# Spreading the expert gates with one single-pass matmul a token, its operands built four tokens at a time

## The chip, the cores and the metric

The kernel runs on one core of one Trainium2 chip. The metric is the device time of one execution in microseconds (us), lower is better. A profile is one execution taken by the hardware profiler; its span is counted from the first to the last instruction. Engines are named as in the profile: PE is TensorE's matmul, PEld its weight load, DVE is VectorE, ACT is ScalarE, POOL is GpSimd and SP is the engine that issues most DMAs.

## What is computed

Three layers over 256 tokens of width 2048. The change lies in the last one, a mixture of 16384 experts, each a row of `u` and a row of `v`. An expert has two keys of 128 values, and each of eight heads picks 16 experts for a token:

```python
cand_s = (v_half[:, :, 0, :, None] + v_half[:, :, 1, None, :]).reshape(T, PEER_HEADS, K * K)
cand_i = (i_half[:, :, 0, :, None] * PEER_N_KEYS + i_half[:, :, 1, None, :])...
top_s, pick = lax.top_k(cand_s, K)
experts = jnp.take_along_axis(cand_i, pick, axis=-1)
gates = jax.nn.softmax(top_s, axis=-1)
...
a = jnp.einsum('cd,ced->ce', hc, w_u[ec]).astype(F32)
coef = (gc * jax.nn.gelu(a)).astype(dt)
return jnp.einsum('ce,ced->cd', coef, w_v[ec])
```

All inputs are float32, and the 128 picks of a token (8 heads by 16) are spread over all 16384 experts.

## The kernel before

The kernel doesn't gather experts. It computes `gelu(h u)` for all of them, multiplies by a dense table of gates that is zero for experts not picked, and multiplies by all of `v`.

**Weights.** A unit of weights is a tile of 128 x 2048 floats, loaded by SP into `raw` (3 buffers). `wsplit` (lines 199 to 230) splits it in two pieces of 1024 columns into an exact high part `whi` (ACT, L210) and a low part `wlo` (DVE, L211), with three buffers for each. Every product is three matmuls on those parts (`mm3`, L289 to L291 for `u`, L285 to L287 for `v`). `wsplit` traces its instructions at high priority.

**Order of the last layer.** The function `peer` works in two halves of the second key (`hf`). A half takes 64 units of `u`, then `apply_gates` for eight blocks of eight units, then 64 units of `v`. The result tiles of the first half fill the slots that the second half's `u` needs, so no unit of the second half comes before the `v` products of the first.

**Spread work.** During the `u` units of the first half a generator `spread` runs in steps, five steps for four units: first `topk`, which leaves `gsel`, a tile [128, 3, 256] with gate, first key and second key of each pick, picks in the partitions and tokens along the columns; then `scatter`, 32 steps of eight tokens. A step's instructions are queued behind the newest split (ACT, DVE) and the newest product (PE) by `anchored`; POOL has no such anchor. Engines take their instructions in the order in which the scheduler of the framework left them.

**Scatter.** For each token it builds two 128 x 128 matrices: on DVE (L1351) a one at the first key of each pick times the gate, on POOL (L1354) a one at the second key. A float32 matmul of one by the other (L1363) sums the picks into a 128 x 128 table in PSUM. Four tokens share a bank; ACT (L1365) copies it into the tile `sg`, and after 16 tokens SP writes `sg` to `gd` in DRAM (L1367). `apply_gates` reads `gd` back by blocks of experts (L1373) and multiplies on POOL (L1377). `coefficients` then splits the result into high and low parts (L1476 on ACT, L1477 on DVE) for the `v` products.

Of the kernel before, what the change touches and what calls it, by code (L numbers as in the profile page):

```python
# [10 lines left out]
F32 = mybir.dt.float32  # L11
# [9 lines left out]
P = 128  # L21
# [7 lines left out]
# columns of the packed per-partition vectors  # L29
V_PRE = 0            # norm_pre, 2 x 16  # L30
V_BQ = 32            # b_q_norm, 2 x 4
V_BKV = 40           # b_kv_norm, 2 x 2
V_BADA = 44          # b_ada, 96
V_GMIX = 140         # g_norm_mix, 16
V_GFFN = 156         # g_norm_ffn, 16
V_PEK = 172          # cmp_pe_k, 16 (j) x 2 (parity)
V_PEV = 204          # cmp_pe_v
V_N = 236

# columns of the packed constants  # L40
C_COSA = 0           # 2 x 128
C_SINA = 256
C_COSB = 512         # 2 x 64
C_SINB = 640
C_CMP = 768          # 2 x 240
C_ROW = 1248         # 2 (rows of the query tiles that see a compressed block)
C_BLK = 1250         # 4
C_IOTA = 1254        # 128
# [3 lines left out]
class Kern:  # L52
# [36 lines left out]
    @contextmanager  # L89
    def phase(self, name, ntmp):  # L90
        """a pool for the temporaries of one phase"""
        self.ntmp = ntmp
        with self.tc.tile_pool(name=name, bufs=1) as self.xp:
            yield
# [9 lines left out]
    def constants(self, lo, hi, eng=None):  # L104
        """the columns lo..hi of the packed constants; returns a way to name them"""
        t = self.xp.tile([P, hi - lo], F32, tag="con", name=self.name("con"))
        (eng or self.nc.gpsimd).dma_start(t, self.a["con"][:, lo:hi])
        return lambda c, n: t[:, c - lo : c - lo + n]

# [1 line left out]
    # prep: generators, a step a unit; heads: generators of three stages, run as a pipeline.  # L111
    # Each step goes behind the newest split of weights and the newest product, so that
    # its inputs are there by the time that the engines come to it.
    def behind(self, *ins):
        """queues what follows behind these instructions, each on its own engine"""
        e = ExitStack()
        for i in ins:
            e.enter_context(self.tc.issue_after(i.ins))
        return e
# [31 lines left out]
    def need(self, key):  # L151
        """runs what is left of the spread work until a result is there"""
        while key not in self.done:
            assert self.prep or self.heads or self.live, key
            self.prep_step()
            self.heads_step()

# [1 line left out]
    def rsqrt(self, out, x, scale, n, eps=EPS):  # L159
        """out = 1/sqrt(x*scale + eps) for [P, n]: a guess from the bits, then Newton steps"""  # L160
# [33 lines left out]
    def wsplit(self, ap, n=2048):  # L194
        """a unit of weights as exact high and low parts, in pieces of at most 1024 columns"""
# [57 lines left out]
    def ada_plan(self, rate, stop):  # L253
        """so many units of the modulation for each unit of weights, up to a number"""
# [6 lines left out]
    def ada_vec(self, i, tag):  # L261
        """mod part i, [128, 16]: feature k*128+p at [p, k]"""
# [6 lines left out]
    def row_bcast(self, out, v, *qs):  # L269
        """out[p, k*128+f] = v[f, k] for every p"""  # L270
# [22 lines left out]
    def proj_tok(self, hT, units, width, evac, kt=KT, early=False, before={}):  # L293
        """token-major: out[t, c] for one chunk of columns; units hold several k tiles"""
# [19 lines left out]
    def proj_feat_by_k(self, hT, units, evac):  # L314
        """feature-major: 512 columns; a unit holds four k tiles, so that it starts before all of hT is there"""
# [12 lines left out]
    def proj_feat(self, hT, units, evac):  # L328
        """feature-major: out[c, t] for 128 columns a unit; two units a bank"""
# [12 lines left out]
    def transposes(self, ps, blocks):  # L342
        """in this order"""
# [6 lines left out]
    # ================= the first two layers =================  # L350
# [3 lines left out]
    def chunk_stats(self, st, m, c, src):  # L354
        """the sum of the squares of a chunk of 512 columns"""
# [3 lines left out]
    def norm_stats(self, r, st, m):  # L359
        """r[:, m] = 1/rms of the rows of tile m from the sums over chunks"""  # L360
# [14 lines left out]
    def start(self, x):  # L375
        """the first loads, in the order of their use"""
# [12 lines left out]
    def layer1(self, l, x, rx, dma=None):  # L389
# [7 lines left out]
        def features(c):  # L397
            """4 tiles of hT; behind the last, the sums that 1/rms needs"""
# [58 lines left out]
        def tables():  # L457
            # rope tables with the gains folded in; 1/rms of x as a row over the tokens
# [45 lines left out]
        qk = [self.S(10 + m, [P, D]) for m in range(2)]   # q 1024, k 256, v 256 (A), v 512 (C)  # L504
# [3 lines left out]
        def a_heads(m, src, nh, h0, ti):  # L508
            """1/rms of nh heads into rqa[:, m, h0:], rope into a temporary"""
# [16 lines left out]
        self.prep_step()  # L526
        kv = self.S(12, [P, 2, 2, 512])      # k_nope (4 x 128), v (4 x 128)
# [39 lines left out]
        qT = self.S(4, [P, 2, 4, T])     # nope parts, then rope parts in the first 64 partitions  # L567
# [5 lines left out]
        def b_prep():  # L573
            # rope on the 64 rope columns of each head and on the shared key
# [189 lines left out]
    def gate(self, m, ps, half_r, src, oT, c):  # L764
        """silu(r*ps) * src, transposed into 4 feature tiles of oT; half_r holds r/2"""
# [21 lines left out]
    def rope(self, dst, src, cos, sin, nh, q):  # L787
        """dst = src*cos + swap(src)*sin on [P, nh, 4q]; swap exchanges neighbouring runs of q"""
# [14 lines left out]
    def softmax_pv(self, scores, sc, scp, vs, out, key):  # L803
        """two heads of 256 keys: out[:, 128*j] = softmax(s_j * scale) @ v_j"""
# [38 lines left out]
    # ================= the last layer: mixer =================  # L843
    def modulated(self, x, rx, g, shift, slots):
        """(x/rms * g + shift) transposed, in high and low parts"""
# [25 lines left out]
    def gain(self, i, vcol, tag):  # L871
        """g * (1 + scale)"""
# [7 lines left out]
    def layer2(self, x, rx):  # L880
# [29 lines left out]
        KTt = self.S(12, [P, 4, 2, T])       # k_c, v_c, k_s, k_w; feature-major  # L910
# [234 lines left out]
        def retain(h2):  # L1145
# [19 lines left out]
            pv = po.rearrange("p (c d) -> p c d", c=4)       # (tile, head)  # L1165
# [89 lines left out]
    # ================= the last layer: experts =================  # L1255
    def topk(self, sh, tk, gsel):
        """the 16 best experts of each head, in steps for the time of other work;
        gates and both key indices go to gsel with (head, k) in the partitions"""
# [73 lines left out]
    def top16(self, row, v, i):  # L1332
        """the 16 largest of a row in order, and their indices; the row is spoilt"""
# [7 lines left out]
    def scatter(self, gsel, gd):  # L1341
        """one-hot rows by one-hot columns, summed over (head, k); a step is 8 tokens"""
        nc = self.nc
        sg = None
        for t0 in range(0, T, 4):
            if t0 % 16 == 0:
                sg = self.S(12 + t0 // 16 % 2, [P, P, 16])
            oh = [self.tmp(tag="oh", bufs=5), self.tmp(tag="oh1", bufs=5)]
            for j in range(4):
                w, t = slice(j * P, (j + 1) * P), slice(t0 + j, t0 + j + 1)  # L1350
                nc.vector.tensor_scalar(  # L1351
                    oh[0][:, w], self.io, gsel[:, 1, t], gsel[:, 0, t], op0=ALU.is_equal, op1=ALU.mult
                )
                nc.gpsimd.tensor_scalar(oh[1][:, w], self.io, gsel[:, 2, t], None, op0=ALU.is_equal)  # L1354
            self.scatter_mm(gd, t0, oh, sg)
            if t0 % 8 == 4:
                yield
    def scatter_mm(self, gd, t0, oh, sg):
        nc = self.nc
        ps = self.pt()  # L1360
        for j in range(4):
            w = slice(j * P, (j + 1) * P)
            nc.tensor.matmul(ps[:, w], oh[0][:, w], oh[1][:, w], start=True, stop=True)  # L1363
        t = t0 % 16
        nc.scalar.copy(sg[:, :, t : t + 4], ps.rearrange("p (t i) -> p i t", t=4))  # L1365
        if t == 12:
            nc.sync.dma_start(gd[t0 // 16], sg.rearrange("p i t -> p (i t)"))  # L1367

    def apply_gates(self, gd, b, A):
        """multiplies 8 tiles of experts by their gates"""  # L1370
# [8 lines left out]
    def peer(self, x, rx, out):  # L1379
# [42 lines left out]
        # gates by (first key, second key) for every token  # L1422
# [7 lines left out]
        for hf in range(2):  # L1430
# [41 lines left out]
            def coefficients(b, j):  # L1472
                ch = self.tmp(dt=F32R, tag="oh", bufs=5)
                cl = self.tmp(dt=F32R, tag="oh1", bufs=5)
# [10 lines left out]
            def finish(n, ms=(0, 1)):  # L1485
                w = slice(n * 512, n * 512 + 512)
                for m in ms:
                    if hf == 0:
                        # the sum of this half, kept until the other is there
# [15 lines left out]
            for b in range(8):  # L1505
                if hf == 1 and b in (1, 3):
                    # x + gate * (the sum of the first half)
# [14 lines left out]
            # the last units by chunks, so that the chunks end one after another  # L1522
# [215 lines left out]
```

## Time and profile before

| | us |
|---|---|
| median of three runs | 3018.02 |
| lowest and highest | 3017.7, 3020.57 |
| span of the profiled execution | 3020.2 |

No time outside the span is given for the profiled execution; its span lies 2.2 us above the median of the runs. In the profile a row of an engine's groups gives the line, the engine, what is written and read, the count, the busy time, the mean of one instruction, and the idle time of the engine in front of it with what ended it. A wait that an engine has while another sets the pace costs nothing.

### The profile page before, as it was taken

Reading aid. Unit: us, or ns where it says so; the run is one execution under the profiler, and the core shown is the slowest. Engines: PE = TensorE matmul, PEld = TensorE weight load, DVE = VectorE, ACT = ScalarE, POOL = GpSimd, SP = SyncE. Lnnn points to the kernel's source line nnn. Section 1 sums busy time; section 2 is a strip of 40 time slices with the busy share of each in tenths; the row PEclk is TensorE's granted clock in tenths of the full one; section 3 lists DMA queues with packets and bytes.
Section 4 is the critical chain, followed back from the end, with each engine's and each line's share of the span. In section 5 each row is a group of like instructions: output and inputs, shape, how many; then the busy total and the mean of one; then the engine's idle time right before and its main releaser. Section 6 shows DMA issues by size and latency. Waiting matters only on the chain.

```text
span 3020.2 us, 45455 instructions
## 1 busy us (share of the span) xinstructions
PE 2942.8 (97%) x18244; PEld 2631.1 (87%) x18244; DVE 1982.9 (66%) x3152; ACT 1366.1 (45%) x1903; POOL 408.1 (14%) x404
## 2 busy tenths in 40 slices
PE   9999989999989999999999998999999999999998
PEld 7798878898879998879999998888889999977886
DVE  6877767867666667856888665655546655555555
ACT  6444445544453455444444444344444443444443
POOL 0000000000030000011018994200000101011001
PEclk9999999999989999999999999999999999999999
DMA  7767757677757656654555557655558677555554
GB/s 277 262 224 287 264 189 269 228 262 280 264 183 273 237 203 226 227 205 162 179 182 182 207 212 237 223 191 185 191 191 294 246 254 264 214 202 209 184 192 139
DMA packets 131955, 672.08 MB, mean 223 GB/s; under 512 B 11200, under 2 KB 44112, under 8 KB 56480
## 3 DMA queue, kind: packets, MB, share of 16 engines
q1 hardware_dynamic: 128384, 650.94, 60.6%
q0 software_dynamic: 3360, 18.24, 1.6%
q8 instruction: 144, 2.36, 0.3%
q14 instruction: 67, 0.55, 0.0%
HBM read 639.77 MB, written 29.36 MB: 222 GB/s over the span
## 4 chain that ended last, share of the span: by engine, by line
PE 88%; DVE 5%; POOL 2%; DMA 2%; issue 2%; ACT 1%; SPq 0%; ACTq 0%; DVEq 0%; POOLq 0%
PE ps L286 16%; PE ps L287 16%; PE ps L285 16%; PE ps L291 11%; PE ps L289 11%; PE ps L290 10%; DVE wlo L211 2%; PE ps L346 2%; DMA raw<-in_wada 2%; PE ps L1363 2%; POOL S L1313 1%; PE ps L833 1%; POOL tmp L1354 1%; ACT whi L210 1%; PE ps L644 0%
## 5 line engine op out<-in xcount | busy, mean ns | idle before, releaser
L211 DVE TENSOR_TENSOR wlo<-raw,whi 128x1024 fp32r<-128x1024 f32 (+2 forms) x950 | 1202.3, 1271 | 800.4 <-ACT whi L210 798.4
L210 ACT CAST whi<-raw 128x1024 fp32r<-128x1024 f32 (+2 forms) x950 | 984.0, 1037 | 1331.0 <-PE ps L287 662.5
L291 PE MATMUL ps<-S,wlo 128*128 128x256 f32 x3072 | 871.5, 284 | 17.2 <-DVE wlo L211 17.0
L289 PE MATMUL ps<-S,whi 128*128 128x256 f32 x3072 | 878.4, 286 | 1.3 <-ACT whi L210 1.3
L290 PE MATMUL ps<-S,whi 128*128 128x256 f32 x3072 | 869.9, 283 | 0.0
L291 PEld LDWEIGHTS ps<-S,wlo 128*128 128x128 f32 x3072 | 590.1, 192 | 19.7 <-DVE wlo L211 19.6
L289 PEld LDWEIGHTS ps<-S,whi 128*128 128x128 f32 x3072 | 590.1, 192 | 6.2 <-issue 4.3
L290 PEld LDWEIGHTS ps<-S,whi 128*128 128x128 f32 x3072 | 590.3, 192 | 0.4
L285 PE MATMUL ps<-whi,S 128*128 128x512 f32 (+3 forms) x1264 | 488.5, 387 | 0.7 <-ACT S L781 0.7
L286 PE MATMUL ps<-wlo,S 128*128 128x512 f32 (+3 forms) x1264 | 482.4, 382 | 3.6 <-DVE wlo L211 3.4
L287 PE MATMUL ps<-whi,S 128*128 128x512 f32 (+3 forms) x1264 | 482.1, 382 | 0.2 <-DVE S L782 0.2
L286 PE MATMUL ps<-wlo,tmp 128*128 128x512 f32 x1024 | 405.4, 396 | 7.4 <-DVE wlo L211 7.3
L285 PE MATMUL ps<-whi,tmp 128*128 128x512 f32 x1024 | 405.1, 396 | 0.0
L287 PE MATMUL ps<-whi,tmp 128*128 128x512 f32 x1024 | 405.0, 395 | 0.0
L286 PEld LDWEIGHTS ps<-wlo,S 128*128 128x128 f32 x1264 | 239.6, 190 | 46.7 <-DVE wlo L211 5.0
L285 PEld LDWEIGHTS ps<-whi,S 128*128 128x128 f32 x1264 | 239.3, 189 | 45.0 <-issue 3.0
L287 PEld LDWEIGHTS ps<-whi,S 128*128 128x128 f32 x1264 | 239.0, 189 | 44.6 <-DVE S L782 0.6
L249 DVE SCALAR_TENSOR_TENSOR raw<-raw,S 128x2048 f32<-128x2048 f32 x96 | 219.6, 2288 | 55.1 <-DMA raw<-in_wada 54.9
L286 PEld LDWEIGHTS ps<-wlo,tmp 128*128 128x128 f32 x1024 | 192.5, 188 | 55.3 <-DVE wlo L211 9.1
L285 PEld LDWEIGHTS ps<-whi,tmp 128*128 128x128 f32 x1024 | 192.5, 188 | 46.3
L287 PEld LDWEIGHTS ps<-whi,tmp 128*128 128x128 f32 x1024 | 192.5, 188 | 46.3
L1354 POOL TENSOR_SCALAR tmp<-con,gsel 128x128 f32<-128x128 f32 x256 | 192.8, 772 | 11.0 <-DVE gsel L1329 7.4
(248 smaller groups left out, 1957.6 us busy)
## 6 DMA issues: line engine op xcount, KB each, us to landing
raw<-in_win SPq DMA_DIRECT2D x136, 1024.0 KB, 5.1
raw<-in_u SPq DMA_DIRECT2D x128, 1024.0 KB, 4.9
raw<-in_v SPq DMA_DIRECT2D x120, 1024.0 KB, 4.9
raw<-in_wada SPq DMA_DIRECT2D x96, 1024.0 KB, 5.0
raw<-in_wout SPq DMA_DIRECT2D x48, 1024.0 KB, 4.9
raw<-in_wq SPq DMA_DIRECT2D x16, 1024.0 KB, 4.9
gd<-S SPq DMA_DIRECT2D x16, 1024.0 KB, 4.5
S<-gd SPq DMA_DIRECT2D x16, 1024.0 KB, 8.3
```

The costliest lines, as they stand in the source:

```text
L210: ia = nc.scalar.copy(hi[:, :h], raw[:, c : c + h])
L211: iv = nc.vector.tensor_sub(lo[:, :h], raw[:, c : c + h], hi[:, :h])
L249: nc.vector.scalar_tensor_tensor(raw, raw, 0.5, self.cact, op0=ALU.mult, op1=ALU.mult, accum_out=self.mod[:, u : u + 1])
L285: mm(out, ah, wh, start=first, stop=False)
L286: mm(out, ah, wl, start=False, stop=False)
L287: self.last_mm = mm(out, al, wh, start=False, stop=last)
L289: mm(out, wh, ah, start=first, stop=False)
L290: mm(out, wh, al, start=False, stop=False)
L291: self.last_mm = mm(out, wl, ah, start=False, stop=last)
L346: t = self.nc.tensor.transpose(ps[:, i * P : (i + 1) * P], b, self.ident)
L1354: nc.gpsimd.tensor_scalar(oh[1][:, w], self.io, gsel[:, 2, t], None, op0=ALU.is_equal)
L1363: nc.tensor.matmul(ps[:, w], oh[0][:, w], oh[1][:, w], start=True, stop=True)
```

## The change

`scatter` gives its matrices other contents and builds them four tokens at a time. The gate is first split into two parts, `hi` rounded to the short float32 form that the matmul takes in one pass, and the rest. Rows are now plain ones at the first key (DVE, 128 x 512 for four tokens), `cols` plain ones at the second key (DVE, 128 x 512). The columns are multiplied by the first gate part on DVE and by the second on POOL (two instructions of 128 x 256 on each), side by side. A token's matmul is then 128 columns of rows by 256 columns, in the form `F32R`. A bank holds two tokens with two sums each; ACT copies one half into `sg` and DVE adds the other to it (128 x 256 each, two of each for four tokens). `scatter_mm` is gone. The tag `oh1` has four buffers where it had five, in `coefficients` too. All other changed lines are comments.

```diff
     def scatter(self, gsel, gd):
...
         nc = self.nc
+        gp = self.xp.tile([P, 2, T], F32, tag="gp", name="gp")
+        hi = self.tmp(dt=F32R, tag="oh", bufs=5)[:, :T]
+        nc.scalar.copy(hi, gsel[:, 0])
+        nc.scalar.copy(gp[:, 0], hi)
+        nc.vector.tensor_tensor(gp[:, 1], gsel[:, 0], gp[:, 0], op=ALU.subtract)
+        io = self.io.rearrange("p (o k) -> p o k", o=1).to_broadcast([P, 4, P])
...
         sg = None
         for t0 in range(0, T, 4):
             if t0 % 16 == 0:
                 sg = self.S(12 + t0 // 16 % 2, [P, P, 16])
-            oh = [self.tmp(tag="oh", bufs=5), self.tmp(tag="oh1", bufs=5)]
-            for j in range(4):
-                w, t = slice(j * P, (j + 1) * P), slice(t0 + j, t0 + j + 1)
-                nc.vector.tensor_scalar(
-                    oh[0][:, w], self.io, gsel[:, 1, t], gsel[:, 0, t], op0=ALU.is_equal, op1=ALU.mult
-                )
-                nc.gpsimd.tensor_scalar(oh[1][:, w], self.io, gsel[:, 2, t], None, op0=ALU.is_equal)
-            self.scatter_mm(gd, t0, oh, sg)
+            ts = slice(t0, t0 + 4)
+            rows = self.tmp(dt=F32R, tag="oh", bufs=5)
+            cols = self.tmp(tag="oh1", bufs=4)
+            parts = [self.tmp(dt=F32R, tag=g, bufs=n) for g, n in (("oh", 5), ("oh1", 4))]
+            nc.vector.tensor_tensor(
+                rows.rearrange("p (t k) -> p t k", t=4), io, over(gsel[:, 1, ts]), op=ALU.is_equal
+            )
+            cv = cols.rearrange("p (t k) -> p t k", t=4)
+            nc.vector.tensor_tensor(cv, io, over(gsel[:, 2, ts]), op=ALU.is_equal)
+            for h in range(2):
+                pv = parts[h].rearrange("p (t e k) -> p t e k", t=2, e=2)
+                for e, eng in enumerate((nc.vector, nc.gpsimd)):
+                    g = gp[:, e, t0 + 2 * h : t0 + 2 * h + 2].rearrange("p (t o) -> p t o", o=1)
+                    eng.tensor_tensor(pv[:, :, e], cv[:, 2 * h : 2 * h + 2], g.to_broadcast([P, 2, P]), op=ALU.mult)
+            t = t0 % 16
+            for h in range(2):
+                ps = self.pt()
+                for j in range(2):
+                    nc.tensor.matmul(
+                        ps[:, j * T : (j + 1) * T], rows[:, (2 * h + j) * P : (2 * h + j + 1) * P],
+                        parts[h][:, j * T : (j + 1) * T], start=True, stop=True,
+                    )
+                pv = ps.rearrange("p (t e i) -> p i t e", t=2, e=2)
+                out = sg[:, :, t + 2 * h : t + 2 * h + 2]
+                nc.scalar.copy(out, pv[:, :, :, 0])
+                nc.vector.tensor_tensor(out, pv[:, :, :, 1], out, op=ALU.add)
...
             if t0 % 8 == 4:
                 yield
-    def scatter_mm(self, gd, t0, oh, sg):
-        nc = self.nc
-        ps = self.pt()
-        for j in range(4):
-            w = slice(j * P, (j + 1) * P)
-            nc.tensor.matmul(ps[:, w], oh[0][:, w], oh[1][:, w], start=True, stop=True)
-        t = t0 % 16
-        nc.scalar.copy(sg[:, :, t : t + 4], ps.rearrange("p (t i) -> p i t", t=4))
...
             def coefficients(b, j):
                 ch = self.tmp(dt=F32R, tag="oh", bufs=5)
-                cl = self.tmp(dt=F32R, tag="oh1", bufs=5)
+                cl = self.tmp(dt=F32R, tag="oh1", bufs=4)
```

## Rows read from the trace of the kernel before

**Rows 1.** The page's busy times, share of the span in brackets.

```profile
PE 2942.8 (97%) x18244; PEld 2631.1 (87%) x18244; DVE 1982.9 (66%) x3152; ACT 1366.1 (45%) x1903; POOL 408.1 (14%) x404
```

**Rows 2.** Busy time by stretch, from the gates' arrival to the first `v` product.

```profile
core 0: us, PE busy (x) PEld busy (x) DVE busy (x) ACT busy (x) POOL busy (x), PEclk, DMA share, GB/s
1631.00:1839.00 208.00, 207.67 (x1764) 207.10 (x1764) 138.16 (x311) 95.20 (x130) 192.80 (x256) 1.00 0.57 211
...
1631.00:1904.00 273.00, 262.33 (x2193) 261.16 (x2193) 176.30 (x333) 118.05 (x157) 218.18 (x262) 0.97 0.62 219
```

**Rows 3.** Groups by line and shape, 1630 to 1840 us.

```profile
L1354 POOL TENSOR_SCALAR tmp<-con,gsel 128x128 f32<-128x128 f32 x256 | 192.8, 772 | 11.0 <-DVE gsel L1329 7.4 <-PE ps L1363 3.6
L1351 DVE TENSOR_SCALAR tmp<-con,gsel 128x128 f32<-128x128 f32 x256 | 78.8, 369 | 2.6 <-PE ps L1363 2.6
L211 DVE TENSOR_TENSOR wlo<-raw,whi 128x1024 fp32r<-128x1024 f32 x53 | 65.0, 1226 | 67.2 <-ACT whi L210 67.2
L1365 ACT COPY S<-ps 128x512 f32<-128x512 f32 x64 | 36.1, 587 | 8.7 <-PE ps L1363 8.7
```

**Rows 4.** The chain that ended last, two steps of the scatter (start, us, what).

```profile
1662.13 1.78 PE ps L1363 x16
1669.67 1.78 PE ps L1363 x16
```

**Rows 5.** Timeline of PE at the end of the first half's `u`.

```profile
1901.77 0.28 PE L289 MATMUL ps<-S,whi 128*128 128x256 f32 x1
1901.89 0.28 PE L290 MATMUL ps<-S,whi 128*128 128x256 f32 x1
...
1903.56 0.40 PE L285 MATMUL ps<-whi,tmp 128*128 128x512 f32 x1
```

**Rows 6.** Two-input DVE groups of the whole run, by line and shape.

```profile
L1268 DVE TENSOR_TENSOR S<-S 128x256 f32<-128x256 f32 x16 | 6.4, 415 | 0.0
L1239 DVE TENSOR_TENSOR S<-S,tmp 128x512 f32<-128x512 f32 x8 | 5.5, 688 | 0.1
L1153 DVE TENSOR_TENSOR tmp<-ps,S 128x256 f32<-128x256 f32 x8 | 3.3, 414 | 0.0
```

**Rows 7.** Instructions of POOL's L1313, a two-input multiply of 128 x 256.

```profile
L1313 POOL TENSOR_TENSOR S<-S,S x32: 728/1167/2785, 1577.5 to 1623.1; 128x256 f32<-128x256 f32 x32
```

**Rows 8.** Timeline of DVE and POOL while POOL runs sixteen of L1313.

```profile
1575.04 2.29 DVE L1305 TENSOR_TENSOR S<-S,con 128x2048 f32<-128x2048 f32 x1
...
1582.27 2.72 DVE L1305 TENSOR_TENSOR S<-S,con 128x2048 f32<-128x2048 f32 x1
1584.91 5.12 DVE L211 TENSOR_TENSOR wlo<-raw,whi 128x1024 fp32r<-128x1024 f32 x3
...
1577.47 20.02 POOL L1313 TENSOR_TENSOR S<-S,S 128x256 f32<-128x256 f32 x16 [207.55 <-DVE S L1305]
```

**Rows 9.** Timeline from the last write of the gates to their use.

```profile
1839.23 0.33 SPq L1367 DMA_DIRECT2D gd<-S  x1
...
1853.99 5.69 POOL L1377 TENSOR_TENSOR S<-S,S 128x2048 f32<-128x2048 f32 x1 [26.38 <-ACT whi L210]
...
1859.72 2.18 ACT L1476 CAST tmp<-S 128x512 fp32r<-128x512 f32 x4 [5.78 <-POOL S L1377]
...
1860.05 4.56 POOL L1377 TENSOR_TENSOR S<-S,S 128x2048 f32<-128x2048 f32 x1 [0.36 <-DMA S<-gd]
...
1860.37 10.89 DVE L1477 TENSOR_TENSOR tmp<-S,tmp 128x512 fp32r<-128x512 f32 x4 [5.17 <-ACT tmp L1476]
```

**Rows 10.** Timeline of DVE in a scatter stretch (idle before in brackets).

```profile
1660.25 1.22 DVE L211 TENSOR_TENSOR wlo<-raw,whi 128x1024 fp32r<-128x1024 f32 x1 [5.15 <-ACT whi L210]
1661.40 2.13 DVE L1351 TENSOR_SCALAR tmp<-con,gsel 128x128 f32<-128x128 f32 x7
1663.44 1.21 DVE L211 TENSOR_TENSOR wlo<-raw,whi 128x1024 fp32r<-128x1024 f32 x1
1664.58 0.39 DVE L1351 TENSOR_SCALAR tmp<-con,gsel 128x128 f32<-128x128 f32 x1
```

More of the change, by code (lines that the diff above doesn't have):

```diff
@@ L1343, in scatter, with over @@
         nc = self.nc
+        gp = self.xp.tile([P, 2, T], F32, tag="gp", name="gp")
[4 more added lines that the diff above has]
+        io = self.io.rearrange("p (o k) -> p o k", o=1).to_broadcast([P, 4, P])
+        def over(a):
+            return a.rearrange("p (t o) -> p t o", o=1).to_broadcast([P, 4, P])
         sg = None
@@ L1356, in scatter @@
+            if t == 12:
+                nc.sync.dma_start(gd[t0 // 16], sg.rearrange("p i t -> p (i t)"))
             if t0 % 8 == 4:
                 yield
-    def scatter_mm(self, gd, t0, oh, sg):
-        nc = self.nc
-        ps = self.pt()
-        for j in range(4):
-            w = slice(j * P, (j + 1) * P)
-            nc.tensor.matmul(ps[:, w], oh[0][:, w], oh[1][:, w], start=True, stop=True)
-        t = t0 % 16
-        nc.scalar.copy(sg[:, :, t : t + 4], ps.rearrange("p (t i) -> p i t", t=4))
-        if t == 12:
-            nc.sync.dma_start(gd[t0 // 16], sg.rearrange("p i t -> p (i t)"))
```

## The prediction, made before the changed kernel was run

> **What bounds the kernel now.** I read the page first: PE is busy 97% of the span and DVE 66% [rows 1], so PE bounds the whole. Then the stretch in which the scatter runs. From the arrival of the gates at 1631 us to the scatter's end at 1839 us PE is busy 207.67 of 208 us, POOL 192.80 and DVE 138.16 [rows 2]. In the chain that ended last, the scatter's matmuls stand at the end of a unit, 16 pieces in 1.78 us, and 7.54 us after one such group comes the next [rows 4]. So PE sets the pace here, POOL is nearly full behind it, and DVE has 70 us left. The scatter must be complete before the first product with `v`, because the table of gates is read by blocks of experts. That product starts at 1903.56 us, right behind the last one of `u` [rows 5], 64 us after the last write of gates [rows 9]. In these 273 us PE was busy 262.33 and DVE 176.30 [rows 2].
>
> The scatter's end can thus slip without harm, but not far. After the last write, issued at 1839.23, the first gated block comes from POOL at 1859.68, and the first split of its coefficients starts on DVE at 1860.37 [rows 9]. A first `v` product needs about 22 us behind the scatter. The scatter may therefore end as late as 1903.6 - 22 = 1882 us.
>
> **The change, engine by engine.**
>
> PE. Removed are 512 pieces: 32 steps of 1.78 us, 57.0 us [rows 4]. Added are 256 single-pass matmuls of 256 columns. The `u` products have that shape and form and start 0.12 us apart [rows 5]: 30.7 us. PE's work falls by 26.3 us, on the path as long as PE sets the pace.
>
> DVE. Removed are 256 instructions of L1351, 78.8 us [rows 3]. Added for every four tokens are two of 128 x 512 with two inputs (688 ns by L1239) and two of 128 x 256 for the first gate part (415 ns by L1268), then two adds of 128 x 256 from PSUM (414 ns by L1153) [rows 6]. That is 1.38 + 0.83 + 0.83 = 3.03 us, one after another. Instructions that don't depend on each other overlap: the split of 1.22 us at 1660.25 is followed by a start 1.15 us later [rows 10], 0.07 us less. With all six overlapping it is 2.6 us. Most wait for something just made (the products for `cols`, the adds for ACT), so I give the overlap to two and take 2.9 us. 64 groups make 186 us, between 166 and 194. Three new instructions ahead of the loop cost about 1 us; they and the two copies of `gsel` count as 3. The adds write pairs of floats 64 bytes apart, which no DVE row here does; ACT's scattered copy of 128 x 512, at 587 ns [rows 3], shows no sign of a price, and I take none.
>
> DVE also keeps the splits. 53 of them took 65.0 us in the scatter stretch, 1.226 us each [rows 3]. A unit is two pieces, and PE works 48 matmuls at 0.12 us [rows 5] on it, 5.76 us. Of PE's 262.33 us up to the first `v` product [rows 2] 57.0 are the scatter's; the remainder is 36 units (207 us), so 72 pieces, of which I count 70 (the first are already there): 86 us.
>
> POOL. Removed are 256 of L1354, 192.8 us [rows 3]. Added are 128 multiplies of 128 x 256. The nearest row is L1313, 0.728 us at least and 1.167 in the median [rows 7]: 93 to 149 us. POOL gets lighter, but what it does now collides with DVE. While sixteen of L1313 ran, DVE's L1305 took 2.72 instead of 2.29 us, three splits took 5.12 (1.71 each instead of 1.226), and POOL itself 1.25 an instruction instead of 0.73 [rows 8]. Per instruction of POOL that costs DVE 0.43 / (2.72 / 1.25) = 0.20 us by L1305 and 0.48 / (1.71 / 1.25) = 0.35 us by the splits. I take 0.27, the middle: 128 x 0.27 = 35 us. The lower bound is nothing, if POOL always gives way; the upper is that DVE waits out all of POOL's 0.73 us, 93 us.
>
> ACT. One copy of 128 x 512 (587 ns [rows 3]) becomes two of half that size. At the full price for each that is 39 us more, and ACT was idle 113 of 208 us [rows 2]. It costs nothing unless ACT is late for the adds; the 22 us at the end hardly change.
>
> Sum for DVE: 3 + 186 + 86 + 35 = 310 us of work from 1631 us, to be done by 1882 to 1904 us if nothing is to be lost. DVE ends it at 1941 us. DVE replaces PE as the bound of this stretch, and PE's 26 us are worth nothing.
>
> What is last then? Splits go ahead of waiting scatter work: at 1663.44 one runs between the seventh and the eighth L1351 of a step [rows 10]. So PE gets its `u` units about as fast as it can take them (207 + 31 us: 1869 us), and the remainder of the scatter comes last, with nothing for PE behind it, since the second half's `u` needs slots that `v` frees. The first `v` product is at 1941 + 22 = 1963 us instead of 1903.6: 60 us later. Behind it the order is as before. Before, PE lost some 10 us to the four L1477 that took 10.89 us beside POOL's gating [rows 9]; that comes back behind the scatter and is inside the 22 us or close to it. I leave it out.
>
> The four instead of five buffers of `oh1` allow `coefficients` two units less of lead. Their instruction came once in two units and had PE's time of two units to hide in; with that cover gone it would cost some tenths of a microsecond each. I take nothing.
>
> So 3020.2 + 60 = 3080 us for the profiled execution. This is 2.2 us above the median of the runs, so 3078 for the median.
>
> **Rivals.**
>
> *Balanced.* Splits give way to the scatter, so that both end together at 1941 us with the gates 22 us earlier: the product comes at 1941, +37 us, 3055. Against it stands the split that cut in [rows 10]. With the low prices (166 and 0.20 a piece) it is 1912, +8.
>
> *A whole lock.* DVE and POOL exclude each other for a whole instruction. For it: four L1477 of about 0.69 us alone by L1239 took 10.89 us while POOL's L1377 of 4.56 us ran [rows 6, 9], so they waited out whole instructions. Against it: the 0.20 to 0.35 above. If DVE pays POOL's full 0.73 us 128 times, it is 93 instead of 35 us, +118 in all: 3136. This is a rule of the Trainium skill, SBUF — State Buffer, section "Who interferes with whom": a DVE instruction with two SBUF inputs contends with a GpSimd instruction that reads SBUF, and the one that issues first blocks the other to its end. The waits of L1477 agree with it; by it the changed kernel, which puts the second input on most of these DVE instructions, would take up to 3136 us.
>
> *No overlap.* The instructions of DVE stand in such an order that every four tokens run through alone: rows and columns 1.38, two multiplies of POOL 2.33, matmul 0.28, copy 0.59, add 0.41, together 5.0 us; 64 of them with the splits give 3 + 320 + 86 = 409 us, +159: 3177. Two groups of buffers in `oh1` speak against it, and the splits that run in the gaps.
>
> *Faster.* DVE just holds the pace. Before, it was idle 97 of the 273 us [rows 2], and at the lowest price the change adds 166 - 79 = 87. If POOL costs it nothing and it never waits, DVE is done at 1631 + 3 + 166 + 86 = 1886, within 4 us of the allowed end, and PE's 26.3 us are gained: 2992. The point that decides is 2.6 us of DVE for four tokens, everything included.
>
> *The matmul is not a single pass.* Then PE would gain nothing. The 0.12 us of the `u` products in the same form [rows 5] exclude it.
>
> **How the numbers follow.** A measurement of this kernel tells about 0.2% (6 us) from no change. Chances: my forecast with the scatter last 0.50 (own range 3055 to 3105), balanced 0.17, whole lock 0.13, no overlap 0.07, faster 0.09, and 0.04 for a case between balanced and faster within 6 us. Of the balanced case, with low prices, 0.02 may end faster as well and 0.01 within 6 us. So faster 0.11, same 0.05, slower 0.84. The range runs from 3020, where DVE's low prices meet a balanced order, to 3140, just beyond the whole lock; it leaves out faster and no overlap, and some of no change, together about 0.2.
>
> **What would show it.** In the changed profile DVE should be busy over 90% from 1631 us to the last write of gates, and that write come near 1941 us. PE should wait for gates between about 1870 and 1963 us, with `v` starting there. The groups on DVE should have 0.69 and 0.41 us for 512 and 256 columns, more where POOL runs; POOL's multiply 0.73 to 1.25 us. The scatter's matmuls should be 256 at 0.12 us. I am wrong if DVE's share stays under 80% while PE waits (then it is the order, not the work), if the adds cost much more than 0.41 us, or if the write comes before 1882 us.

## The result and the profile after

The changed kernel takes 3101.8 us (median of 4 runs, 3100.9 to 3103.9) where the kernel before takes 3017.9: the ratio is 1.0277, with a 95% interval of 1.0264 to 1.0289. It is 84 us slower. The forecast was 3078 us, 60 us slower. The profiled execution's span grew from 3020.2 to 3098.9 us, by 78.7.

The page's busy times after, which answer to [rows 1]:

```profile
PE 2959.6 (96%) x17988; PEld 2630.0 (85%) x17988; DVE 2115.3 (68%) x3281; ACT 1373.4 (44%) x1969; POOL 332.3 (11%) x276
```

Over the whole span nothing much has moved: DVE has 132 us more, POOL 76 us less. The stretches tell more. These are the windows of the changed kernel with the columns of [rows 2]: from the gates' arrival to the last write of gates, and from there to just behind the first `v` product.

```profile
1631.00:1917.00 286.00, 224.51 (x1543) 208.61 (x1542) 268.34 (x439) 104.41 (x196) 116.10 (x128) 0.85 0.44 155
1917.00:1985.00 68.00, 61.04 (x436) 57.85 (x435) 44.37 (x24) 25.95 (x31) 29.30 (x6) 0.92 0.86 266
```

The scatter takes 286 us instead of 208. DVE is busy 268 of them, 94%; PE, full before, is idle 61.5. PE's own work did shrink: 1543 pieces instead of 1764. But the clock that was granted to it fell from 1.00 to 0.85 of full speed while it waited so often. Of the 1287 products of `u` in the stretch 138 start 0.21 us apart instead of 0.12, which is the lower of the two levels (1.2 GHz of 2.4); they come after PE has waited.

The groups of DVE in that stretch, by line and shape (busy us, mean ns; then the idle time before them), which answer to [rows 3]:

```profile
L211 DVE TENSOR_TENSOR wlo<-raw,whi 128x1024 fp32r<-128x1024 f32 x54 | 70.1, 1297 | 10.2 <-ACT whi L210 9.6
L1373 DVE TENSOR_TENSOR tmp<-tmp,gp 128x256 fp32r<-128x256 f32 x128 | 69.2, 569 | 1.8
L1364 DVE TENSOR_TENSOR tmp<-con,gsel 128x512 fp32r<-128x512 f32 x64 | 55.1, 861 | 0.0
L1385 DVE TENSOR_TENSOR S<-ps,S 128x256 f32<-128x256 f32 x128 | 48.5, 414 | 5.5 <-ACT S L1384 5.4
L1368 DVE TENSOR_TENSOR tmp<-con,gsel 128x512 f32<-128x512 f32 x64 | 43.5, 679 | 0.0
```

The columns (L1368, 679 ns) and the adds (L1385, 414 ns) cost what the nearest rows said. The rows (L1364), of the same shape as the columns, take 861 ns, and the multiplies (L1373) 569 instead of 415. Both run beside POOL's multiply. Busy time of groups counts overlaps twice: these five add up to 286.4 us, DVE's busy time is 268.3.

The waits of that stretch (us in total, times, the longest):

```profile
POOL tmp L1373 <- DVE tmp L1368: 136.0, 52, 10.5
...
ACT S L1384 <- PE ps L1378: 71.6, 53, 4.0
PE ps L1378 <- POOL tmp L1373: 55.2, 35, 4.0
```

POOL waits 136 us for the columns that DVE makes, and PE 55 us for POOL. POOL's work is light now (116 us of 286); it is late because DVE is late, and PE because POOL is. The timeline of all engines shows one turn of this loop:

```profile
1787.58 0.68 DVE L1368 TENSOR_TENSOR tmp<-con,gsel 128x512 f32<-128x512 f32 x1
1788.29 1.18 DVE L1373 TENSOR_TENSOR tmp<-tmp,gp 128x256 fp32r<-128x256 f32 x2
1788.40 1.54 POOL L1373 TENSOR_TENSOR tmp<-tmp,gp 128x256 fp32r<-128x256 f32 x2 [3.42 <-DVE tmp L1368]
...
1789.24 1.55 PE L1378 MATMUL ps<-tmp,tmp 128*128 128x256 f32 x4 [3.36 <-POOL tmp L1373]
1789.39 1.10 DVE L1364 TENSOR_TENSOR tmp<-con,gsel 128x512 fp32r<-128x512 f32 x1
...
1790.02 0.39 ACT L1384 COPY S<-ps 128x256 f32<-128x256 f32 x1 [3.23 <-PE ps L1378]
1790.44 0.42 DVE L1385 TENSOR_TENSOR S<-ps,S 128x256 f32<-128x256 f32 x1
...
1791.57 0.68 DVE L1368 TENSOR_TENSOR tmp<-con,gsel 128x512 f32<-128x512 f32 x1
```

From one L1368 to the next it is 3.99 us. DVE works in almost all of it, on four tokens; PE does four matmuls and waits. No split falls into this turn. That is so in 24 of the 63 turns; the others have one or two.

Of the 78.7 us of span, 69.6 are there when `v` starts: the last write of gates comes at 1916.94 instead of 1839.23 (+77.7), and the first `v` product at 1973.13 instead of 1903.56, 56 us behind the write instead of 64. The other 9.2 us come later, in lines that the diff doesn't touch.

```profile
1916.94 0.42 SPq L1387 DMA_DIRECT2D gd<-S  x1
...
1934.15 4.63 POOL L1400 TENSOR_TENSOR S<-S,S 128x2048 f32<-128x2048 f32 x1 [20.64 <-DMA S<-gd]
...
1973.13 0.40 PE L285 MATMUL ps<-whi,tmp 128*128 128x512 f32 x1
```

### The profile page after: what moved, and what is told of

Its sections match the earlier page's. It is cut to its first block, busy times and chain, and to the rows that moved or that the text cites. A ratio compares the mean times of both kernels' runs of the same rounds, so it can differ in the third digit from the quotient of the medians.

```text
span 3098.9 us, 44960 instructions
## 1 busy us (share of the span) xinstructions
PE 2959.6 (96%) x17988; PEld 2630.0 (85%) x17988; DVE 2115.3 (68%) x3281; ACT 1373.4 (44%) x1969; POOL 332.3 (11%) x276
## 4 chain that ended last, share of the span: by engine, by line
PE 83%; DVE 8%; DMA 3%; issue 2%; POOL 2%; ACT 2%; SPq 0%; ACTq 0%; POOLq 0%; DVEq 0%
PE ps L286 15%; PE ps L287 15%; PE ps L285 15%; PE ps L291 10%; PE ps L289 10%; PE ps L290 10%; DVE wlo L211 4%; DMA raw<-in_wada 2%; PE ps L346 2%; PE ps L1378 1%; PE ps L833 1%; ACT whi L210 1%; POOL tmp L1373 1%; POOL S L1313 1%; DVE tmp L1368 1%
## 5 line engine op out<-in xcount | busy, mean ns | idle before, releaser
L290 PE MATMUL ps<-S,whi 128*128 128x256 f32 x3072 | 876.8, 285 | 0.0
L291 PEld LDWEIGHTS ps<-S,wlo 128*128 128x128 f32 x3072 | 597.0, 194 | 18.8 <-DVE wlo L211 18.8
L289 PEld LDWEIGHTS ps<-S,whi 128*128 128x128 f32 x3072 | 597.8, 195 | 6.8 <-issue 4.3
L290 PEld LDWEIGHTS ps<-S,whi 128*128 128x128 f32 x3072 | 597.5, 194 | 0.4
L1400 POOL TENSOR_TENSOR S<-S,S 128x2048 f32<-128x2048 f32 x16 | 81.4, 5089 | 726.1 <-DVE raw L249 473.1
```

Source lines behind the costliest of these rows:

```text
L289: mm(out, wh, ah, start=first, stop=False)
L290: mm(out, wh, al, start=False, stop=False)
L291: self.last_mm = mm(out, wl, ah, start=False, stop=last)
L1400: nc.gpsimd.tensor_tensor(av, av, gb.rearrange("p g i t -> p i g t"), op=ALU.mult)
```

## The experiments

The expectations name three theories. Theory 1: the amount of DVE's work sets the length of the stretch. Theory 2: the loop of a group of tokens through DVE, POOL, PE and ACT does, whoever is busy. Theory 3: DVE waits for POOL where both read SBUF, and that is the cost. All kernels start from the changed one unless it is said otherwise, each time is the median of four to ten runs, and "over before" is that median less the one of the kernel before on the same chip (3017.9 to 3019.5). Where two kernels are compared below, it is by "over before". DVE's busy time is that from 1631 us to the last write of gates.

| kernel | us | over before | ratio, 95% | DVE busy / stretch |
|---|---|---|---|---|
| changed | 3101.8 | +84.0 | 1.0264 to 1.0289 | 268.3 / 286 |
| rows once | 3050.2 | +31.9 | 1.0082 to 1.0128 | 215.4 / 234 |
| no add | 3074.9 | +56.6 | 1.0168 to 1.0211 | 237.2 / 251 |
| second part on ACT | 3072.3 | +54.0 | 1.0155 to 1.0200 | 230.2 / 254 |
| deeper buffers | 3092.7 | +74.0 | 1.0222 to 1.0275 | 258.8 / 276 |
| second part on ACT, no add | 3031.8 | +12.3 | 1.0024 to 1.0047 | 187.3 / 215 |
| operands built once | 2997.1 | -21.7 | 0.9918 to 0.9951 | 110.9 / 190 |
| before, single pass only | 3007.9 | -10.4 | 0.9950 to 0.9976 | 136.7 / 196 |
| single pass, POOL relieved | 2989.6 | -29.1 | 0.9887 to 0.9920 | 148.2 / 179 |
| before, exact mix | 3031.2 | +11.8 | 1.0026 to 1.0047 | 179.1 / 221 |

**Rows once.** The one-hot rows are made once, ahead of the loop, and every token uses them.

```diff
+        rows = self.tmp(P, dt=F32R, tag="rows", bufs=1)
+        nc.vector.tensor_scalar(rows, self.io, gsel[:, 1, 0:1], None, op0=ALU.is_equal)
...
-            nc.vector.tensor_tensor(
-                rows.rearrange("p (t k) -> p t k", t=4), io, over(gsel[:, 1, ts]), op=ALU.is_equal
-            )
```

> The one-hot rows are built once, for one token, and used for all (part left out: the rows of all other tokens). DVE loses 64 instructions of 128 x 512 (55 us busy); POOL's multiply, the matmuls, the copies and the adds stay, and so does the chain through them. Theory 1, DVE's amount of work sets the length of the scatter: 50 to 58 us less than the changed kernel's 3101.8, so 3044 to 3052. Theory 2, the chain columns, POOL, matmul, copy, add through few buffers sets it and DVE only looks full: at most 8 us less, 3094 or more.

It is 52 us faster than the changed kernel. The window to the last write:

```profile
1631.00:1865.00 234.00, 200.59 (x1529) 196.08 (x1528) 215.44 (x375) 101.64 (x196) 120.14 (x128) 0.91 0.51 189
```

DVE has 52.9 us less to do, the stretch is 52 us shorter and the kernel 52. DVE is still busy 92% of it. This is theory 1, microsecond for microsecond. The rows that are gone had 55.1 us (64 times 861 ns).

**No add.** The second part's product is computed and not added.

```diff
                 nc.scalar.copy(out, pv[:, :, :, 0])
-                nc.vector.tensor_tensor(out, pv[:, :, :, 1], out, op=ALU.add)
```

> The adds of the second sum are dropped (part left out: the second gate part's contribution). DVE loses 128 instructions, 48.5 us busy. Theory 1 (DVE's work): 45 to 52 us less, 3050 to 3057. Theory 2 (chain): the loop of 4.0 us for four tokens loses one add of 0.41 us and a semaphore, some 0.45 x 64 = 29 us, 3073.

It is 27 us faster, about theory 2's number and well short of theory 1's. But DVE is busy 237 of 251 us, 94%, which theory 2 would not have it be: of the 48.5 us taken from it only 31 are gone. The window, and then the groups of DVE that grew:

```profile
1631.00:1882.00 251.00, 208.66 (x1515) 200.12 (x1514) 237.19 (x311) 101.95 (x196) 104.13 (x128) 0.88 0.50 174
```

```profile
L211 DVE TENSOR_TENSOR wlo<-raw,whi 128x1024 fp32r<-128x1024 f32 x52 | 76.5, 1471 | 7.1 <-ACT whi L210 7.1
L1373 DVE TENSOR_TENSOR tmp<-tmp,gp 128x256 fp32r<-128x256 f32 x128 | 75.1, 627 | 6.5
```

Splits went from 1297 to 1471 ns and multiplies from 569 to 627. Without the adds in between, DVE's two-input instructions meet POOL's multiplies more often. So a number that fitted theory 2 came from theories 1 and 3 together; a run without POOL had to tell.

**Second part on ACT.** POOL's 128 multiplies become 256 copies by ACT with the gate as a scale.

```diff
-                for e, eng in enumerate((nc.vector, nc.gpsimd)):
-                    ...
+                g = gp[:, 0, t0 + 2 * h : t0 + 2 * h + 2].rearrange("p (t o) -> p t o", o=1)
+                nc.vector.tensor_tensor(pv[:, :, 0], cv[:, 2 * h : 2 * h + 2], g.to_broadcast([P, 2, P]), op=ALU.mult)
+                for j in range(2):
+                    q = t0 + 2 * h + j
+                    nc.scalar.activation(pv[:, j, 1], cv[:, 2 * h + j], AF.Copy, scale=gp[:, 1, q : q + 1])
```

> The columns times the second gate part are made by ACT (256 instructions of 128 x 128 with a scale per partition) instead of POOL (128 of 128 x 256). DVE's instructions stay the same. Theory 3, POOL's two-input multiplies hold DVE up: DVE's mean durations fall to 0.68 (512 columns), 0.41 (256 columns) and 1.23 us (split), which is 34 us less of DVE, so 3068. Without that effect: no gain from DVE, and ACT's 256 x 0.3 = 77 us on top of 104 in 286 us might delay splits: 3100 to 3115.

It is 30 us faster. The window, and the groups of DVE in it:

```profile
1631.00:1885.00 254.00, 213.07 (x1518) 204.55 (x1518) 230.22 (x438) 177.60 (x451) 0.00 (x0) 0.88 0.47 173
```

```profile
L211 DVE TENSOR_TENSOR wlo<-raw,whi 128x1024 fp32r<-128x1024 f32 x53 | 64.8, 1224 | 17.0 <-ACT whi L210 16.3
L1372 DVE TENSOR_TENSOR tmp<-tmp,gp 128x256 fp32r<-128x256 f32 x128 | 49.2, 421 | 1.2
L1387 DVE TENSOR_TENSOR S<-ps,S 128x256 f32<-128x256 f32 x128 | 48.3, 420 | 5.5 <-ACT S L1386 4.4
L1364 DVE TENSOR_TENSOR tmp<-con,gsel 128x512 fp32r<-128x512 f32 x64 | 43.9, 686 | 0.0
L1368 DVE TENSOR_TENSOR tmp<-con,gsel 128x512 f32<-128x512 f32 x64 | 43.9, 686 | 0.0
```

With POOL silent, the same instructions of DVE have the durations of [rows 6] again. The price of sharing with POOL is the difference of the groups: 69.2 - 49.2 = 20 us on the multiplies, 55.1 - 43.9 = 11 on the rows, and 54 x 0.073 = 4 on the splits, together 35 us, or 0.27 us for each of POOL's 128 instructions. Theory 3 is right in size, and it works through theory 1: DVE has 38 us less to do. Only 30 are gained. PE now waits 37 us for ACT, which has taken POOL's place; that this wait keeps back the other 8 is likely and not shown.

**Second part on ACT, no add.** The two edits above together: without POOL, do the adds give back their full price?

> The run with the second product on ACT (3072), without the adds (part left out: the second gate part's contribution). There is no POOL work left to meet DVE. If DVE's amount of work sets the time and the adds gave back only 27 of their 48.5 us because the freed DVE met POOL more often, they give back 42 to 50 us here: 3022 to 3030. If the chain of products, matmul, copy and add sets it, some 29 us again: 3043.

```profile
1631.00:1846.00 215.00, 198.50 (x1507) 194.21 (x1506) 187.26 (x310) 174.33 (x451) 0.00 (x0) 0.93 0.56 202
```

It is 42 us faster than with the adds, and DVE has 43 us less to do. Theory 2's 29 is out. The time, 3031.8, lies 2 us above the range of theory 1. What had kept back part of the gain in the run without the adds was POOL.

**Deeper buffers.** The rows get buffers of their own, so that more groups can be under way.

```diff
-            rows = self.tmp(dt=F32R, tag="oh", bufs=5)
-            cols = self.tmp(tag="oh1", bufs=4)
+            rows = self.tmp(dt=F32R)
+            cols = self.tmp(tag="oh", bufs=5)
```

> The changed kernel with more buffers in flight: rows in four idle temporaries, columns beside the first parts in five, second parts alone in four; all work is the same. Theory 1 (DVE's amount of work): DVE was busy 268 of 286 us, so at most 18 us less; I expect 0 to 10 less than 3101.8, 3092 to 3102. Theory 2 (two groups in flight make the chain of columns, POOL, matmul, copy, add the bound): 25 us less or more, 3077.

It gains 10 us, with 9.6 us less of DVE's busy time (258.8 us): the rows no longer meet POOL's multiplies (680 ns instead of 861), splits and multiplies meet them a little more (1353 and 586 ns). The 10 us are near the noise: this kernel's runs go from 3086.5 to 3102.5 us, and its interval overlaps that of the changed kernel. Theory 2's 25 us are out; the loop isn't short of buffers.

**Operands built once.** All builds are made once, for the first four tokens, ahead of the loop; matmuls, copies and adds stay for every group (the moved lines are abridged here).

```diff
         sg = None
+        t0 = 0
+        rows, cols, parts = ...
         for t0 in range(0, T, 4):
             ...
-            rows, cols, parts = ...
```

> The operands of the matmuls are built once, for the first four tokens, and used for all 64 groups (part left out: the one-hot operands of all other tokens). Matmuls, copies, adds and writes stay. DVE is left with the splits and the adds (65 + 49 us). Theory 1: PE sets the pace again and the 26 us of PE come out, scatter ends near 1813 us, 2988 to 2996. Rival: the matmul in its new form, its two copies or the adds behind them cost by themselves (the adds are queued in DVE in front of splits): no faster than 3018.

```profile
1631.00:1821.00 190.00, 184.30 (x1527) 182.88 (x1526) 110.85 (x187) 98.03 (x196) 1.61 (x2) 1.00 0.65 234
```

The granted clock is 1.00 again, PE 97% busy, and the kernel 21.7 us faster than before, 1 us short of theory 1's range. So the gain on PE exists, close to the 26.3 us worked out for it; the builds hide it and more.

**Before, single pass only.** The kernel before, with its one-hot tiles in the single-pass type. One 128-column matmul a token, so the gate is rounded and its second part left out.

```diff
-            oh = [self.tmp(tag="oh", bufs=5), self.tmp(tag="oh1", bufs=5)]
+            oh = [self.tmp(dt=F32R, tag="oh", bufs=5), self.tmp(dt=F32R, tag="oh1", bufs=5)]
```

> The kernel before with its two one-hot tiles in the single-pass form, so one matmul of 128 columns a token in place of two pieces (part left out: the second gate part, gates are rounded). DVE, POOL and ACT do what they did before. If a single pass of 128 columns costs 0.06 to 0.12 us, PE's 57 us fall to 15 to 31. If PE alone had set the pace, 26 to 42 us less than before, 2976 to 2992. My theory: POOL with 193 us of work in 208 is next, so at most 15 us less, 3003 to 3012. If 128 columns cost as much as the float32 form, no change.

```profile
1631.00:1827.00 196.00, 189.01 (x1495) 185.90 (x1494) 136.71 (x308) 92.14 (x129) 191.45 (x255) 0.95 0.60 219
```

It gains 10 us, and then POOL with its 256 one-hots is full: 191 of 196 us. That is the engine that stood right behind PE in [rows 2].

**Single pass, POOL relieved.** The same, with one second one-hot in four built by DVE.

```diff
-                nc.gpsimd.tensor_scalar(oh[1][:, w], self.io, gsel[:, 2, t], None, op0=ALU.is_equal)
+                (nc.vector if j == 3 else nc.gpsimd).tensor_scalar(
+                    oh[1][:, w], self.io, gsel[:, 2, t], None, op0=ALU.is_equal
+                )
```

> As the run of the kernel before with single-pass matmuls of 128 columns (part left out: the second gate part, gates are rounded), and one token in four has its second one-hot built on DVE instead of POOL. POOL 192 - 48 = 144 us, DVE 137 + 64 x 0.31 = 157, PE 26.5 units x 5.76 + 256 x 0.10 = 179. If POOL was the bound that took PE's gain, the scatter ends near 1815 us: 2992 to 2998, some 10 to 15 less than that run's 3008. If not: 3005 to 3010.

```profile
1631.00:1810.00 179.00, 179.00 (x1516) 179.00 (x1515) 148.23 (x375) 92.34 (x130) 158.59 (x192) 1.00 0.67 245
```

PE is full at a granted clock of 1.00, and the kernel is 29 us faster than before, 2 us better than the range: the best of all here, with rounded gates.

**Before, exact mix.** Both gate parts and 256 columns, with the builds spread: POOL makes the rows, DVE the columns times the first part in one instruction with one tensor input, ACT scales them to the second part (`gp[:, 1]` is divided by the first part ahead of the loop).

```diff
+                nc.gpsimd.tensor_scalar(rows[:, j * P : (j + 1) * P], self.io, gsel[:, 1, q], None, op0=ALU.is_equal)
...
+                    pv[:, 0], self.io, gsel[:, 2, q], gp[:, 0, q], op0=ALU.is_equal, op1=ALU.mult
...
+                nc.scalar.activation(pv[:, 1], pv[:, 0], AF.Copy, scale=gp[:, 1, q])
```

> Both gate parts, single-pass matmuls of 256 columns and the adds as in the changed kernel, but built a token at a time: POOL makes the one-hot rows (as before, 192 us), DVE columns times the first part in one instruction (79 us), ACT the second part from the first by a scale per partition (82 us). DVE 65 + 79 + 49 = 193, POOL 192, ACT 56 + 45 + 82 = 183, PE 183. If the amount of work on the fullest engine sets the time, the scatter takes some 195 to 205 us instead of 208: 3005 to 3018. If engines this full wait for each other in turn, 3020 to 3045.

```profile
1631.00:1852.00 221.00, 201.36 (x1505) 196.16 (x1504) 179.06 (x438) 173.12 (x449) 190.49 (x255) 0.92 0.55 196
```

It is 72 us faster than the changed kernel and still 12 us slower than the one before. No engine is full, but four are at 78 to 91%, and they wait for each other. No version with both gate parts was found that beats the kernel before.

## Why the prediction came out as it did

**PE's saving** was right, and so was that it would be worth nothing. The matmul is single-pass: eight of L1378 take 1.11 us at full clock, of which the last's own 0.28 leaves 0.12 for each of the others. Without the builds the kernel is 21.7 us faster.

**DVE as the new bound** was right: 94% busy until the last write, as the prediction asked for. Four edits show that a microsecond of DVE is about a microsecond of the kernel: 52.9 less gave 52, 31 gave 27, 38 gave 30, and 43 on top of the 38 gave 42.

**DVE's price for four tokens** was taken as 2.9 us and is 2.6, the lower bound. Without POOL, DVE is busy 230.2 us, less the 64.8 of the splits 165.4, which is 2.58 us for each of the 64 groups: all six instructions overlap, not two. This term was 20 us too large.

**The collision with POOL** was 35 us in the sum and is 35 by the runs. What it is made of can be read in the timeline. Two narrow windows at the turn shown above part the pairs:

```profile
1788.40 0.79 POOL L1373 TENSOR_TENSOR tmp<-tmp,gp 128x256 fp32r<-128x256 f32 x1 [3.42 <-DVE tmp L1368]
...
1788.63 0.83 DVE L1373 TENSOR_TENSOR tmp<-tmp,gp 128x256 fp32r<-128x256 f32 x1
1789.15 0.79 POOL L1373 TENSOR_TENSOR tmp<-tmp,gp 128x256 fp32r<-128x256 f32 x1
```

POOL's first ends at 1789.19 and DVE's multiply of 256 columns 0.27 us later; POOL's second ends at 1789.94 and DVE's L1364 of 512 columns, at 1790.49, 0.55 us later. Twice the columns, twice the time: DVE does its columns after POOL's end, and its record holds the wait. The whole stretch bears this out. 89 of DVE's instructions are over 0.05 us longer than with POOL silent, and each has the end of one of POOL's 128 within it: 50 of 256 columns end 0.28 us behind it, 28 of 512 columns 0.55 us, and 11 splits of 1024 columns 1.08 us. So the rival of a whole lock was right about the mechanism. The Trainium skill has this in SBUF — State Buffer, section "Who interferes with whom": a DVE instruction with two SBUF inputs contends with a GpSimd instruction that reads SBUF, the shared ports are an exclusive lock, and the order of issue decides who blocks. The trace agrees with 0.27 and 0.55 us. What the rival had wrong is the price. DVE comes when POOL is already at work and pays the remainder, 0.42 us for each of POOL's two in such a turn (1.18 us for two multiplies that take 0.76 with POOL silent, 1.10 for the rows that take 0.69), and over the whole stretch 0.27 on average, since only these 89 of POOL's 128 cost DVE anything to speak of. The 0.73 us of POOL's whole instruction were never due. That the 0.27 of the sum came out is in part luck: it was the middle between two prices of unlike instructions.

It need not be DVE that pays. In the kernel before, POOL's L1354, with one tensor input, ran beside the same splits for 192.8 of 208 us, and the splits kept their 1.226 us [rows 3]. There POOL paid (shortest, median and longest of its 256, in ns):

```profile
L1354 POOL TENSOR_SCALAR tmp<-con,gsel x256: 591/598/1878, 1631.2 to 1827.0; 128x128 f32<-128x128 f32 x128
```

A split that began with up to 0.38 us of an L1354 still to run lost nothing. An L1354 that began during a split ended 0.47 us behind it in nearly all cases, and took 1.3 us or more.

**The order** is the step that failed: "Splits go ahead of waiting scatter work ... and the remainder of the scatter comes last, with nothing for PE behind it." With it failed the slack, "The scatter may therefore end as late as 1903.6 - 22 = 1882 us." Engines take their instructions in a fixed order, and in it `u` cannot run ahead of the scatter. From 1631 us to the last write DVE does 54 splits; before it did 53, and in the nine other kernels it does 52 to 54. Behind the scatter's last matmul, PE still has nine units of `u` to do before the first `v` product, or eight and a half in the changed kernel, whose last four scatter matmuls come a little later in the order. One of the three lines of those products (L290, 16 matmuls a unit) shows it, before and after; its first number in brackets is the count:

```profile
1838.40:1903.50 65.10, 41.62 (x144) 28.73 (x144) 0.90 0.77 244
1914.40:1973.00 58.60, 39.37 (x136) 27.18 (x136) 0.91 0.80 251
```

So the 64 us between the last write and `v` in the kernel before were not slack but mostly work that comes after the scatter in any case. In the ten other kernels `v` starts 55 to 61 us behind the last write. With the rows made once the scatter ends well ahead of 1882 us, and `v` still starts 17 us later than before:

```profile
1865.80 0.33 SPq L1385 DMA_DIRECT2D gd<-S  x1
...
1920.54 0.40 PE L285 MATMUL ps<-whi,tmp 128*128 128x512 f32 x1
```

In the changed kernel PE therefore stands in front of the scatter's matmuls again and again, not once at the end: it idles 61.5 us within the stretch, nearly all of it before L1378, instead of 93 us behind its `u`. The balanced rival, which had the write and `u` end together, isn't what happened either.

**Two errors that nearly cancel.** The prediction had 310 us of DVE work before the last write; 268 were there, 20 less by the price of the builds and 20 by 16 splits that come later (54, not 70). DVE also stood idle for 18 us. So the write came at 1917 instead of 1941 us. Behind it came 56 us to the first `v` product instead of 22. The one error takes 24 us off and the other adds 34, so that `v` started at 1973 instead of 1963: that the forecast is this close there is luck.

In PE's own terms: before, 208 us of work. The 1543 pieces of the new stretch are 256 x 0.12 and 1287 / 48 units of 5.76 us, together 185 us at full clock; PE was busy 224.5. So 61.5 us of idle time and 39 us more of busy time, less 23 saved, make the 78 us. Of the 39, 12 are the 138 products of `u` at the lower clock. Some 25 lie in the scatter's own matmuls: from the start of each to the next start or its own end they take 56 us for 256, where 31 were worked out; many stand alone between waits, and how much of this is the clock isn't shown. That a faster PE would only have waited longer is argued from DVE's 94%, not measured.

**ACT and the coefficients** cost next to nothing, as foretold: PE waited 0.3 us in all for the copies (L1384), and DVE 5.4. The four buffers of `oh1` cost nothing that shows: the kernel with operands built once and the exact mix have them too, and from the first `v` product to the end both take 1115 us, where the kernel before takes 1117 and the changed one 1126.

**Left open** are the 9.2 us behind the first `v` product. The second half's `u`, from its first gelu to its last, takes 366.1 us instead of 361.9, and what follows 383.7 instead of 379.0, in unchanged lines; in the other kernels that `u` takes 362 to 375. No experiment was aimed at it. The miss of 24 us (84 for 60) is then 9.6 us at the first `v` product, left over from the two errors, these 9.2, and 5 between the profiled executions (spans 78.7 us apart) and the medians (84).

## What to carry to other kernels

Before work is taken off the engine that bounds a stretch, add up what each other engine has to do in the same stretch: here PE gave back 26 us and DVE, with 70 us free, got 130 more, 35 of them waits for POOL. A DVE instruction with two tensor inputs in SBUF can be dearer than its duration alone when a two-input instruction of GpSimd runs beside it, and taking other work off DVE can make them meet more often, as the run without the adds showed. Beside GpSimd's comparisons with one tensor input it was GpSimd that paid, in the kernel before. Time between the end of one engine's work and its use is slack only if nothing queued behind that work has to run in it: here 64 us looked like 43 us of slack, and nine units of `u` stood in them. That is read from the order of instructions in the timeline, not from totals.

## What the runs showed of the hardware that was not expected

- Half the columns hardly shorten a single-pass matmul here. Eight with 256 columns take 1.11 us (changed kernel) and eight with 128 columns 1.00 (before, single pass only); less the last's 0.28 that is 0.12 and 0.10 us for each of the others.
- Two-input DVE instructions that wait for GpSimd show the wait as busy time: a 128 x 256 multiply reads 0.83 us instead of 0.42, so DVE's 94% includes some 35 us of waiting.
- ACT's scaled copy of 128 x 128 takes 0.40 us (second part on ACT), about the time of its plain copy of 128 x 256 (0.39 from PSUM, 0.41 from SBUF): half the columns with a scale save nothing, and 256 of them cost ACT 82 us.
